# A hybrid encoder layer on one core: gate weight splits re-timed, one transfer chain moved to GpSimd's queue, a table load moved, and two token tiles of the closing norm done otherwise

## The chip, the cores and the metric

The kernel runs on one core of a Trainium2 chip. The core has five engines that run their own instruction lists in order and meet at semaphores: TensorE (PE in the profile; PEld is its weight loading), VectorE (DVE), ScalarE (ACT), GpSimd (POOL) and SyncE (SP), which here only issues transfers. Sixteen DMA engines move data between the chip's memory (DRAM) and the core's. The metric is the device time of one execution in microseconds (us); the time of a kernel is the median of its runs.

## The reference

One encoder layer on 1024 tokens of width 1024, all in float32:

```
u = x @ W_in                                  # rq rk rv rg | aq ak av
y_ret = silu(rg) * groupnorm(retention_fwd(rq,rk,rv) + retention_bwd(rq,rk,rv)) * gn_gain   # 8 heads of 64
y_att = windowed attention of aq on ak, av    # 8 query heads, 2 kv heads, +-128 tokens, ALiBi, a sink logit
h = LN1(alpha * x + [y_ret, y_att] @ W_out)
f = (silu(h @ W_gate) * (h @ W_up)) @ W_down + sigmoid(h @ W_pg) * (p @ W_pe)   # hidden width 2816
out = LN2(alpha * h + f)
```

Retention is done in chunks of 128 tokens with a running state of 64x64 for each head and direction; groupnorm takes mean and variance over the 64 numbers of a head. The two layer norms take mean and variance over a token's 1024 numbers, with eps 1e-5, a gain and a bias.

## The kernel before

**Arithmetic.** Float32 products are made from halves: `split` copies a number to its rounded `hi` on ACT (type fp32r) and subtracts to get `lo` on DVE (L71, L72). A product of two split operands is three matmuls, hi*hi, hi*lo and lo*hi (`mm3`, L77 to L79). Later stages use Strassen's seven products for a 2x2 block product, so their weights are needed as sums and differences of blocks, each split in turn.

**Order.** The first part (to about 342 us) is written as a list of steps for PE; TensorE's list follows it, and a scheduler lines up what the other engines get. It runs the input projection as a filler: every triple of projection matmuls is a *tick* (0.68 us of PE). `take(k)` (L283) issues k ticks and, at every tick, those steps whose due tick has come from two lists, `side` and `later`. So a table of ticks says where a side job's instructions fall among the others. A pair of retention heads and the attention heads beside it make a stage; the first retention pair takes 48 ticks (120.5 to 163.1 us), and the second pair, with the second attention pair beside it, the next 48 (163.1 to 221.9 us).

**The gate's splits.** The weight of the embedding gate (W_pg) is needed much later, as seven split block sums for each of four row blocks k. `presplit_gate` (L645) makes them ahead of time in these two stages: `load(k)` (L651, transfers at L653) brings two tiles `pre` of 512 KB; each of seven steps may first add blocks on DVE (L663), then `put` (L601) copies to one of two tiles `pro` on ACT (L602), subtracts on DVE (L603), and stores 512 KB from SP's queue into `pgd` (L604). A step can only begin once the tile `pro` of two steps ago has been stored. `load(2)` goes with the first step of k=1, and `load(3)` has a place of its own in the table `at`.

**Retention's norm.** For each pair i and half hh of the tokens, `norm` (L494) sums squares over heads on PE, and DVE makes a row `kv` of two heads (L500). The reciprocal root is then made in five steps with due ticks 3, 6, 9, 12 and 15 ahead (`LAGS`): `spread` (two transfers of 2 KB that lay the row over partitions, `sn`), `power` on GpSimd (L508), `store` (4 KB to `rnd` in DRAM, L511), `fetch` (two broadcasting transfers of 128 KB into `kv1` or `rb`, L515), and `scaled` on DVE, which multiplies the retention output `y` (L519). All transfers are issued by SP. `qq` and `pt` are key operands, scaled on DVE (L411) and used by PE (L428); the same tiles hold squares (L489, L490 evicts the output).

**Attention.** `scores` makes a block's scores and softmax (`sc`), `turn` transposes them on PE (L572), ACT evicts them to `ptr` (L574), and `values` multiplies with the values (L584).

**The out-projection** follows at about 342 us. Its left operands are sums of the `y` tiles (`H`, `h`, `h0a`, by `split` and by additions at L870 to L876), its weights come split from `wod` by SP (L814). ACT evicts the first products into `h0b` (L972). The retention gate (L722 to L724) closes `y` of the last pair there.

**The feed-forward part** from about 545 us is written in units (`gunits`), with `ahead_g` issuing the preparation of operands for coming units. `post` evicts products to `ev` tiles on ACT (L1424, L1426) or adds them on DVE (L1417), and `finish` applies silu on ACT (L1388) and multiplies on DVE (L1390). ACT holds the functions of one table at a time and has to load another to change (`ACT_TABLE_LOAD`). L1854 calls silu once on one number, which brings a load of its table there; the sigmoid of the embedding gate (L1097) comes after it.

**The tail.** The last products complete token tiles 0 to 3 one after the other (`tail`, L1683); tiles 4 to 7 are finished before, by `ln2_steps`. For tiles 0 to 3 the layer norm on tile `accd[t]` (128 tokens) goes: `addto` adds the last product; with `done` also sums the tile's half, on DVE within the same instruction (L1618) or, for a half that is subtracted into, on ACT (L1624); `var` makes the negative mean (L1630) and squares on ACT (L1635); `rstd` makes the reciprocal root by a power on GpSimd (L1652); `center` subtracts the mean and multiplies by the gain in one DVE instruction per half (L1657); `scale` multiplies by the reciprocal root and adds the bias, again one DVE instruction per half, and stores each half (256 KB) from SP's queue (L1662, L1663). Only tile 3 (`LAST`) takes its statistics by `bn_stats` and `bn_aggr` on DVE (L1622, L1641) instead. Tiles 4 to 7 are scaled on ACT (L1674), multiplied by the gain on DVE (L1677), and their bias is added by an accumulating transfer on GpSimd's queue (L1678).

Of the kernel before, what the change touches and what calls it, by code (L numbers as in the profile page):

```python
# [11 lines left out]
AF = mybir.ActivationFunctionType  # L12
# [10 lines left out]
NPAIR = 4  # L23
# [19 lines left out]
def layer(tc, xT, xn, w_first, w_mt, w_rv, w_out, w_pg, w_pe, pT, w_gu, w_dn,  # L43
# [349 lines left out]
    class Retention:  # L393
# [100 lines left out]
        def norm(self, hh):  # L494

            b = self.o.rearrange("p n c -> p (n c)")
            for k in range(2):
                pe.matmul(b, ones, self.sq[k], start=k == 0, stop=k == 1)
            row = bt([2, HF], "kv0")
            behind(dve.tensor_scalar(row, b[0:2], 1.0 / 64, EPS, ALU.mult, ALU.add))  # L500
            sm, r, home = bt([P, 2, 8], "sn", 1), bt([P, HF], ("kv1", "rb")[hh]), rnd[2 * self.i + hh]

            def spread():
                for h in range(2):
                    sp.dma_start(sm[64 * h:64 * h + 64, 0], row[h:h + 1].rearrange("o (q e) -> o q e", e=8))

            def power():
                behind(pool.tensor_tensor(sm[:, 1], sm[:, 0], cst[:, C_MH:C_MH + 1].to_broadcast([P, 8]), ALU.pow))  # L508

            def store():  # L510
                sp.dma_start(home, sm[:, 1])  # L511

            def fetch():
                for h in range(2):
                    sp.dma_start(r[64 * h:64 * h + 64], home[64 * h:64 * h + 64].rearrange("q e -> (q e)").partition_broadcast(64))  # L515

            def scaled():
                y = self.half(hh)
                behind(dve.scalar_tensor_tensor(y, y, gn[:, self.i:self.i + 1], r, ALU.mult, ALU.mult))  # L519

            later.extend((ticks[0] + at, f) for at, f in zip(LAGS, (spread, power, store, fetch, scaled)))
# [123 lines left out]
    def presplit_gate():  # L645

        first, other = ([a_tile([P, 2, HF], "pre", t) for _ in range(2)] for t in ("A1", "A0"))
        ops = [a_tile([P, 2, HF], "pro", "A1", F32R) for _ in range(2)]
        n = [0]

        def load(k):  # L651
            for j in range(2):
                sp.dma_start((other if k == 1 else first)[j], w_pg[j, k])  # L653

        def steps(k):
            raw = other if k == 1 else first

            (a11, a21), (a12, a22) = ([raw[j][:, i, :] for i in range(2)] for j in range(2))

            def s(p, x, *sums):  # L660
                def f():
                    for a in sums:
                        behind(dve.tensor_tensor(*a))  # L663
                    put(x, ops[n[0] % 2], pgd[p - 1, k])
                    n[0] += 1
                return f

            return [s(1, a11), s(4, a22), s(2, a12), s(5, a22, (a22, a21, a22, ALU.add)),
                    s(7, a21, (a21, a11, a21, ALU.subtract)), s(6, a11, (a11, a22, a11, ALU.subtract)),
                    s(3, a12, (a12, a12, a11, ALU.subtract))]  # L670

        load(0)
        load(1)
        k0, k1, k2, k3 = map(steps, range(4))
        k1[0] = pair_of(k1[0], lambda: load(2))
        k3[0:0] = [lambda: load(3), lambda: None]
        at = [2 + 3.4 * k for k in range(12)] + [55 + 2.5 * k for k in range(2)] + [65 + 1.9 * k for k in range(7)] + \
            [78.5 + 2 * k for k in range(9)]
        return [(ticks[0] + t, f) for t, f in zip(at, k0 + k1 + k2 + k3, strict=True)]

    def pair_of(f, g):
# [932 lines left out]
    def addto(t, h, b, op=ALU.add, done=False):  # L1614


        if done and t != LAST and op == ALU.add:
            dve.tensor_tensor_reduce(half(t, h), half(t, h), b, 1.0, 0.0, op, ALU.add, stts[t][:, h:h + 1])  # L1618
            return
        dve.tensor_tensor(half(t, h), half(t, h), b, op)  # L1620
        if done and t == LAST:
            dve.bn_stats(stts[t][:, 6 * h:6 * h + 6], half(t, h))  # L1622
        elif done:
            act.activation(ct([P, HF], "sg", 2), half(t, h), AF.Copy, accum_out=stts[t][:, h:h + 1])  # L1624

    LAST = 3

    def negmean(t):
        stt = stts[t]
# [7 lines left out]
    def var(t):  # L1637

        stt = stts[t]
        if t == LAST:  # L1640
            dve.bn_aggr(stt[:, 12:14], stt[:, 0:12])  # L1641
            dve.tensor_scalar(stt[:, 12:13], stt[:, 12:13], -1.0, None, ALU.mult)
        else:
            negmean(t)
            squares(t)

    def rstd(t):
        stt = stts[t]
        if t != LAST:
            dve.tensor_scalar(stt[:, 13:14], stt[:, 2:3], stt[:, 3:4], 1.0 / D, ALU.add, ALU.mult)  # L1650
        dve.tensor_scalar(stt[:, 14:15], stt[:, 13:14], EPS, None, ALU.add)
        pool.tensor_tensor(stt[:, 15:16], stt[:, 14:15], cst[:, C_MH:C_MH + 1], ALU.pow)  # L1652

    def center(t):
        for h in range(2):
            x = half(t, h)
            dve.scalar_tensor_tensor(x, x, stts[t][:, 12:13], ln2[0][:, hs[h]], ALU.add, ALU.mult)  # L1657

    def scale(t):
        for h in range(2):  # L1660
            x = half(t, h)
            dve.scalar_tensor_tensor(x, x, stts[t][:, 15:16], ln2[1][:, hs[h]], ALU.mult, ALU.add)  # L1662
            sp.dma_start(out[t][:, hs[h]], x)  # L1663
# [18 lines left out]
    def tail(products):  # L1682

        bs = dbank[len(SEG) - 1, GRP[4]]
        for t in range(4):
            products(t)
            if t:
                rstd(t - 1)
            addto(t, 0, bs[t], done=True)
            var(t)  # L1690
            if t < LAST:
                if t:
                    scale(t - 1)
                center(t)
        rstd(LAST)
        scale(LAST - 1)
        center(LAST)
        scale(LAST)

    GRP = {1: 0, 2: 0, 5: 1, 3: 1, 6: 2, 7: 2, 4: 2}  # L1700

# [137 lines left out]
    with tc.manual_schedule(engines={ET.PE, ET.DVE, ET.Activation, ET.Pool, ET.SP}):  # L1839
        for _ in range(4):  # L1840
            oslots.append(wp.tile([P, 2, HF], F32R, tag="w", bufs=4, name=nm("w")))
            oslots.append(ct([P, 2, HF], "u", 4, F32R))
        sums2.extend(a_tile([P, 2, HF], "sums") for _ in range(2))
        fa = big16((P, 4, 2, 2, Q))
        halves4 = [(fa[:, k, 0], fa[:, k, 1]) for k in range(4)]
        halves4.append(tuple(ct([P, 2, Q], "sg", 2, F32R) for _ in range(2)))
        fsum.extend([cst[:, 0:Q], cst[:, Q:2 * Q], *(ct([P, Q], "fs", 2) for _ in range(2))])
        fwide = ct([P, 2, Q], "p", 2)
        fine, more = fine_right(2, halves4[:3]), fine_right(4, halves4[3:])
        fine += more  # L1850
        homes.update((name, a_tile([P, 2, HF], "ev")) for name in ("spare", "s1", "u2", "c11", "u3", "c22"))
        FINE4 = len(plan(0)) + len(plan(1)) - 2
        FINES = (2, 4, 7, 9, 20, 23, 26, FINE4)
        act.activation(fsum[3][:, 0:1], fsum[0][:, 0:1], AF.Silu)  # L1854
        ahead_g(-1, 4)
        for k in range(NG):
            gunits[k][1]()
            gunits[k][2]()
            if k in FINES:
                at = max([-1] + [i for i, x in enumerate(items) if x.right]) + 1  # L1860
                for x in fine.pop(0):
                    at += 1
                    x.unit, x.right = items[at].unit, True
                    items.insert(at, x)
                    at += 1
            ahead_g(k, k + 1 + min(9, 4 + k))
            while stores and stores[0][0] <= k:
                stores.pop(0)[1]()
            j = k + 1 - NG
            if j == -6:  # L1870
                while items:
                    items.pop(0).issue()
                release()
                arenas_a()
                op_arena(ct([P, 4, 2, HF], "h0a", dt=F32R))
                arena("chain", ct([P, 8, HF], "h0b"), 8)
            if j == -4:
                for _ in range(3):
                    op_arena(big16((P, 4, 2, HF)))
            if j >= -6:  # L1880
                ahead(0, j + 7)
            if j >= -4:
                ahead(1, j + 5)
        arena("b", big.tile([P, 8, HF], F32, tag="H", bufs=4, name=nm("H")), 8)
        arena("chain", ct([P, 8, HF], "h2"), 8)
        op_arena(ct([P, 4, 2, HF], "h3", dt=F32R), 4)
        rings["op"] += [ct([P, 2, HF], "u", 4, F32R) for _ in range(2)]
        for k in range(ND):
            d_step(k)
# [83 lines left out]
```

## Time and profile before

| | us |
|---|---|
| runs | 1169.49, 1171.92, 1171.9 |
| median | 1171.9 |
| profiled execution, its own time | 1172.7 |
| its span | 1170.6 |
| granted TensorE clock, mean | 0.998 |

The profile is of one execution. An engine's busy time says little here: PE is nearly always busy, and what is left are the places where it waits, the start, and the end of the span where PE has finished. A timeline row gives start, length, engine, line, operation, output<-inputs, shapes and how many rows it joins, and in brackets the idle time ahead of it with what ended it. `pgd`, `wod`, `rnd`, `ped` are places in DRAM; `w<-wod` is a transfer from there.

### The profile page before, as it was taken

Reading aid. Unit: us, or ns where it says so; the run is one execution under the profiler, and the core shown is the slowest. Engines: PE = TensorE matmul, PEld = TensorE weight load, DVE = VectorE, ACT = ScalarE, POOL = GpSimd, SP = SyncE. Lnnn points to the kernel's source line nnn. Section 1 sums busy time; section 2 is a strip of 40 time slices with the busy share of each in tenths; the row PEclk is TensorE's granted clock in tenths of the full one; section 3 lists DMA queues with packets and bytes.
Section 4 is the critical chain, followed back from the end, with each engine's and each line's share of the span. In section 5 each row is a group of like instructions: output and inputs, shape, how many; then the busy total and the mean of one; then the engine's idle time right before and its main releaser. Section 6 shows DMA issues by size and latency. Waiting matters only on the chain.

```text
span 1170.6 us, 17933 instructions
## 1 busy us (share of the span) xinstructions
PE 1156.5 (99%) x6330; PEld 971.5 (83%) x6330; DVE 900.4 (77%) x1746; ACT 580.1 (50%) x1181; POOL 121.0 (10%) x181
## 2 busy tenths in 40 slices
PE   9999999999999999999999999999999999999996
PEld 7888888788887888888888888888888888888885
DVE  4666688777869688947998988888888976773677
ACT  5566348686756256214445434443344445552463
POOL 2001021202010021000000000000000020133232
PEclk9999999999999999999999999999999999999999
DMA  6345665746356955665322222232223289999977
GB/s 252 100 153 207 246 207 193 244 159 223 127 190 230 365 172 196 261 195 201 117 90 105 112 105 100 102 135 101 99 72 136 89 249 349 350 225 203 261 173 216
DMA packets 84378, 213.86 MB, mean 183 GB/s; under 512 B 12225, under 2 KB 17473, under 8 KB 84289
## 3 DMA queue, kind: packets, MB, share of 16 engines
q1 hardware_dynamic: 75648, 195.94, 47.6%
q0 software_dynamic: 8640, 16.78, 8.2%
q8 instruction: 50, 0.82, 0.3%
q14 instruction: 40, 0.32, 0.1%
HBM read 141.32 MB, written 62.16 MB: 174 GB/s over the span
## 4 chain that ended last, share of the span: by engine, by line
PE 86%; DVE 6%; DMA 4%; ACT 2%; issue 1%; POOL 0%; SPq 0%; DVEq 0%; ACTq 0%; POOLq 0%
PE bmm L803 8%; PE bmm L804 8%; PE bmm L805 7%; PE bt L803 6%; PE bt L804 6%; PE bt L805 6%; PE bmm L77 4%; PE bs L803 4%; PE bs L805 4%; PE bs L804 4%; PE bmm L79 4%; PE bmm L78 4%; PE bo L805 3%; PE bo L803 3%; PE bo L804 3%
## 5 line engine op out<-in xcount | busy, mean ns | idle before, releaser
L77 PE MATMUL bmm<-H,w 128*128 128x512 f32 x240 | 97.3, 405 | 0.0
L78 PE MATMUL bmm<-H,w 128*128 128x512 f32 x240 | 93.9, 391 | 0.0
L79 PE MATMUL bmm<-H,w 128*128 128x512 f32 x240 | 93.9, 391 | 0.0
L1388 ACT ACTIVATE ev<-ev 128x512 f32<-128x512 f32 x42 | 26.5, 630 | 104.3 <-DVE ev L1417 92.8
L1562 POOL DMA_DIRECT2D h0b<-in_w_dn x24 | 21.6, 899 | 540.7 <-DVE ev L1368 504.9
L77 PEld LDWEIGHTS bmm<-H,w 128*128 128x128 f32 x240 | 45.1, 188 | 11.1 <-issue 1.4
L79 PEld LDWEIGHTS bmm<-H,w 128*128 128x128 f32 x240 | 45.1, 188 | 10.3
L78 PEld LDWEIGHTS bmm<-H,w 128*128 128x128 f32 x240 | 45.2, 188 | 7.9
L554 ACT ACTIVATE sc<-sc,st 128x385 f32<-128x385 f32 (+1 forms) x64 | 37.2, 585 | 15.6 <-DVE st L552 15.3
L550 DVE CUSTOM_DVE_ANT_0 sc<-cst,bs,skb 128x384 f32<-128x384 f32 (+1 forms) x64 | 35.0, 575 | 8.3 <-PE bs L549 7.8
L1417 DVE TENSOR_TENSOR ev<-ev,bt 128x512 f32<-128x512 f32 x44 | 30.1, 683 | 12.5 <-PE bt L805 12.5
L1368 DVE TENSOR_TENSOR ev<-ev,bs 128x256 f32<-128x256 f32 x63 | 25.6, 418 | 15.5 <-PE bs L805 14.7
L1390 DVE TENSOR_TENSOR ev<-ev 128x512 f32<-128x512 f32 x42 | 29.0, 691 | 10.5 <-ACT ev L1388 9.0
L803 PE MATMUL bmm<-H,u 128*128 128x512 f32 x92 | 36.2, 393 | 0.2 <-ACT ev L1426 0.2
L804 PE MATMUL bmm<-H,u 128*128 128x512 f32 x92 | 36.0, 392 | 0.0
L805 PE MATMUL bmm<-H,u 128*128 128x512 f32 x92 | 35.8, 389 | 0.0
L72 DVE TENSOR_TENSOR w<-raw,w 128x512 fp32r<-128x512 f32 x34 | 23.1, 688 | 16.2 <-ACT w L71 16.1
L545 POOL COPY sc<-skb 128x1 f32<-128x1 f32 x64 | 15.6, 253 | 188.9 <-PE bt L572 144.5
L560 ACT ACTIVATE sc<-sc,st 128x384 f32<-128x384 f32 (+1 forms) x64 | 34.2, 580 | 1.2 <-DVE st L558 0.9
L71 ACT ACTIVATE H<-ln 128x512 fp32r<-128x512 f32 (+1 forms) x34 | 22.7, 675 | 21.2 <-DVE ln L1052 7.2
L803 PE MATMUL bmm<-H,w 128*128 128x512 f32 x84 | 32.9, 392 | 0.0
L804 PE MATMUL bmm<-H,w 128*128 128x512 f32 x84 | 32.9, 392 | 0.0
(802 smaller groups left out, 3898.4 us busy)
## 6 DMA issues: line engine op xcount, KB each, us to landing
ad<-ev SPq DMA_DIRECT2D x33, 512.0 KB, 2.6
pgd<-pro SPq DMA_DIRECT2D x28, 512.0 KB, 3.0
raw<-in_w_gu SPq DMA_DIRECT2D x22, 512.0 KB, 3.6
ln<-in_w_gu SPq DMA_DIRECT2D x22, 512.0 KB, 3.9
raw<-ad SPq DMA_DIRECT2D x40, 256.0 KB, 5.6
ln<-ad SPq DMA_DIRECT2D x37, 256.0 KB, 6.0
H<-in_w_dn SPq DMA_DIRECT2D x33, 256.0 KB, 7.4
wod<-aq SPq DMA_DIRECT2D x15, 512.0 KB, 2.8
```

The costliest lines, as they stand in the source:

```text
L77: pe.matmul(o, lh, rh, start=start, stop=False)
L78: pe.matmul(o, lh, rl, start=False, stop=False)
L79: recent[0] = pe.matmul(o, ll, rh, start=False, stop=stop).ins.name
L550: dve.tensor_tensor_reduce(sc[g][:, :nk], cst[:, tc0:tc0 + nk], b[:, :nk], slope(i, g), skb[:, 2 * i + g:2 * i + g + 1], ALU.add, ALU.max, ...
L554: act.activation(sc[g][:, :nk + 1], sc[g][:, :nk + 1], AF.Exp, bias=st_[:, 1, j, g:g + 1], accum_out=st_[:, 2, j, g:g + 1])
L560: behind(act.activation(sc[g][:, :nk], sc[g][:, :nk], AF.Copy, scale=st_[:, 3, j, g:g + 1]))
L803: pe.matmul(o, lh, rh, start=start, stop=False, skip_group_check=True)
L804: pe.matmul(o, lh, rl, start=False, stop=False, skip_group_check=True)
L805: pe.matmul(o, ll, rh, start=False, stop=stop, skip_group_check=True)
L1388: act.activation(c[:, 0, :], c[:, 0, :], AF.Silu)
L1390: dve.tensor_tensor(c[:, 1, :], c[:, 0, :], c[:, 1, :], ALU.mult)
L1417: dve.tensor_tensor(get(name), ev[left][:, m, :], right, ALU.add)
```

## The change

The edits lie in four parts of the kernel. None touches what PE does.

```diff
+            q = pool if hh and self.i == NPAIR - 1 else sp
...
             def store():
-                sp.dma_start(home, sm[:, 1])
+                q.dma_start(home, sm[:, 1])
 
             def fetch():
                 for h in range(2):
-                    sp.dma_start(r[64 * h:64 * h + 64], home[64 * h:64 * h + 64].rearrange("q e -> (q e)").partition_broadcast(64))
+                    q.dma_start(r[64 * h:64 * h + 64], home[64 * h:64 * h + 64].rearrange("q e -> (q e)").partition_broadcast(64))
...
         k3[0:0] = [lambda: load(3), lambda: None]
-        at = [2 + 3.4 * k for k in range(12)] + [55 + 2.5 * k for k in range(2)] + [65 + 1.9 * k for k in range(7)] + \
-            [78.5 + 2 * k for k in range(9)]
+        at = [2 + 2.8 * k for k in range(14)] + [60 + 1.9 * k for k in range(7)] + [73 + 1.9 * k for k in range(9)]
...
-        if done and t != LAST and op == ALU.add:
+        if done and t not in BN and op == ALU.add:
...
-        if done and t == LAST:
+        if done and t in BN:
             dve.bn_stats(stts[t][:, 6 * h:6 * h + 6], half(t, h))
...
-    LAST = 3
+    LAST, BN = 3, (2, 3)
...
         for t in range(4):
             products(t)
-            if t:
+            if t in (1, 2):
                 rstd(t - 1)
             addto(t, 0, bs[t], done=True)
             var(t)
-            if t < LAST:
-                if t:
-                    scale(t - 1)
-                center(t)
-        rstd(LAST)
-        scale(LAST - 1)
-        center(LAST)
-        scale(LAST)
+            if t in BN:
+                rstd(t)
+            if t == 1:
+                scale(0)
+            elif t == 2:
+                act.activation(accd[1], accd[1], AF.Copy, scale=stts[1][:, 15:16])
+                pool.dma_start(accd[1], ln2[1], accum_op=ALU.add)
+            center(t)
+            if t in BN:
+                scale(t)
+            if t == 2:
+                sp.dma_start(out[1], accd[1])
...
-        act.activation(fsum[3][:, 0:1], fsum[0][:, 0:1], AF.Silu)
         ahead_g(-1, 4)
         for k in range(NG):
...
             ahead_g(k, k + 1 + min(9, 4 + k))
+            if k == 0:
+                act.activation(fsum[3][:, 0:1], fsum[0][:, 0:1], AF.Silu)
```

Line numbers in the rows of after are those of the changed file, one to five higher. `var` and `rstd` ask for `t in BN` where they asked for `t == LAST`.

**Gate's splits.** The table has 30 places, counted in ticks from 120.5 us on. Before: 12 from tick 2 to 39.4, two at 55 and 57.5, seven from 65 to 76.4, nine (the first two of them `load(3)` and an empty place) from 78.5 to 94.5. After: 14 from 2 to 38.4, seven from 60 to 71.4, nine from 73 to 88.2. So two of the splits move from the second stage into the first, and the last ends six ticks earlier.

DVE where the second stage hands over to the third, up to the key operand `pt` of the third, before:

```order
L603 TENSOR_TENSOR pro_1168<-pre_1163,pro_1168 128x512
L663 TENSOR_TENSOR pre_1164<-pre_1164,pre_1163 128x512
L519 SCALAR_TENSOR_TENSOR y_1596<-y_1596,gn,kv_2110 128x512
L251 SCALAR_TENSOR_TENSOR aq_2236<-bmm_2242,aq_2236 64x512
L411 TENSOR_TENSOR qq_2330<-bt_2325,kd 128x512
L603 TENSOR_TENSOR pro_1167<-pre_1163,pro_1167 128x512
L251 SCALAR_TENSOR_TENSOR aq_2237<-bmm_2242,aq_2237 64x512
L411 TENSOR_TENSOR qq_2330<-bt_2325,kd 128x512
L603 TENSOR_TENSOR pro_1168<-pre_1164,pro_1168 128x512
L72 TENSOR_TENSOR w_2335<-raw_2333,w_2335 128x512
L72 TENSOR_TENSOR w_2338<-raw_2333,w_2338 128x512
L411 TENSOR_TENSOR pt_2360<-bt_2355,kd 128x512 x2
```

And after:

```order
L665 TENSOR_TENSOR pre_1164<-pre_1164,pre_1163 128x512
L251 SCALAR_TENSOR_TENSOR aq_2249<-bmm_2125,aq_2249 64x512
L605 TENSOR_TENSOR pro_1168<-pre_1164,pro_1168 128x512
L500 TENSOR_SCALAR kv_2288<-bo_2201 2x512
L72 TENSOR_TENSOR w_2335<-raw_2333,w_2335 128x512
L521 SCALAR_TENSOR_TENSOR y_1604<-y_1604,gn,kv_2116 128x512
L411 TENSOR_TENSOR qq_2330<-bt_2325,kd 128x512
L251 SCALAR_TENSOR_TENSOR aq_2248<-bmm_2254,aq_2248 64x512
L411 TENSOR_TENSOR qq_2330<-bt_2325,kd 128x512
L72 TENSOR_TENSOR w_2338<-raw_2333,w_2338 128x512
L251 SCALAR_TENSOR_TENSOR aq_2249<-bmm_2254,aq_2249 64x512
L411 TENSOR_TENSOR pt_2360<-bt_2355,kd 128x512 x2
```

The rows of `pro` and `pre` have moved ahead. From the eviction `y` (L490), which stands further up in both, to `pt` there are 20 rows before and 14 after.

ACT where the second attention block of the second stage has its two transposes evicted (`ptr`, 128x384), before:

```order
L235 ACTIVATE rk_1726<-bmm_1728 128x512
L574 ACTIVATE ptr_1828<-bt_1824 128x384
L560 ACTIVATE sc_1776<-sc_1776,st_1635 128x384
L560 ACTIVATE sc_1777<-sc_1777,st_1635 128x384
L574 ACTIVATE ptr_1834<-bt_1830 128x384
L554 ACTIVATE sc_1836,st_1635<-sc_1836,st_1635 128x385
```

And after:

```order
L235 ACTIVATE rk_1730<-bmm_1732 128x512
L562 ACTIVATE sc_1779<-sc_1779,st_1643 128x384
L562 ACTIVATE sc_1780<-sc_1780,st_1643 128x384
L576 ACTIVATE ptr_1837<-bt_1833 128x384
L604 ACTIVATE pro_1167<-pre_1164 128x512
L576 ACTIVATE ptr_1843<-bt_1839 128x384
L556 ACTIVATE sc_1845,st_1643<-sc_1845,st_1643 128x385
```

Both scalings `sc` and a split (`pro`) now stand ahead of the second eviction, the scalings ahead of the first too.

**The last factor.** Only for the last pair's second half, `store` and `fetch` are issued by GpSimd. SP's list there, before:

```order
L505 DMA sn_3719<-kv_3717 64x1x8 x2
L511 DMA rnd<-sn_3719 128x8
L604 DMA ped<-aq_3046 128x1024
L515 DMA rb_3720<-rnd 64x512 x2
L814 DMA u_3835<-wod 128x1024
L814 DMA w_3837<-wod 128x1024
```

And after:

```order
L507 DMA sn_3719<-kv_3717 64x1x8 x2
L606 DMA ped<-aq_3046 128x1024
L815 DMA u_3835<-wod 128x1024
L815 DMA w_3837<-wod 128x1024
L815 DMA u_3839<-wod 128x1024
```

The weights `wod` follow directly on `ped`; the three transfers of the factor stand on GpSimd's list behind its power. On DVE one of the splits `H<-y,H` now stands ahead of the `y` that takes the factor (L519), and the second of the additions L876 is the 26th row behind `y` where it was the 28th.

**Silu's table.** The one-number silu goes from ahead of all units to behind the first. Before, ACT loads silu's table at L1854, the sigmoid's at L1097 and silu's again at L1388; after, the sigmoid's and then silu's once, between two evictions at L1425.

**The closing norm.** Tile 2 takes its statistics like tile 3, and goes through `center` and `scale` ahead of tile 3. Tile 1 is no longer scaled on DVE: ACT scales it (128x1024), GpSimd's queue adds the bias by an accumulating transfer, and SP stores it whole (512 KB), behind tile 2's stores and ahead of tile 3's. DVE's last rows before:

```order
L1662 SCALAR_TENSOR_TENSOR acc_8948<-acc_8948,stt_3931,u_9976 128x512 x2
L1657 SCALAR_TENSOR_TENSOR acc_8976<-acc_8976,stt_3932,u_9974 128x512 x2
L1650 TENSOR_SCALAR stt_3932<-stt_3932 128x1
L1651 TENSOR_SCALAR stt_3932<-stt_3932 128x1
L1620 TENSOR_TENSOR acc_9000<-acc_9000,bs_9954 128x512
L1622 BN_STATS stt_3933<-acc_9000 128x6
L1641 BN_AGGR stt_3933<-stt_3933 128x2
L1642 TENSOR_SCALAR stt_3933<-stt_3933 128x1
L1651 TENSOR_SCALAR stt_3933<-stt_3933 128x1
L1662 SCALAR_TENSOR_TENSOR acc_8976<-acc_8976,stt_3932,u_9976 128x512 x2
L1657 SCALAR_TENSOR_TENSOR acc_9000<-acc_9000,stt_3933,u_9974 128x512 x2
L1662 SCALAR_TENSOR_TENSOR acc_9000<-acc_9000,stt_3933,u_9976 128x512 x2
```

And after:

```order
L1642 BN_AGGR stt_3932<-stt_3932 128x2
L1643 TENSOR_SCALAR stt_3932<-stt_3932 128x1
L1652 TENSOR_SCALAR stt_3932<-stt_3932 128x1
L1658 SCALAR_TENSOR_TENSOR acc_8976<-acc_8976,stt_3932,u_9974 128x512 x2
L1663 SCALAR_TENSOR_TENSOR acc_8976<-acc_8976,stt_3932,u_9976 128x512 x2
L1621 TENSOR_TENSOR acc_9000<-acc_9000,bs_9954 128x512
L1623 BN_STATS stt_3933<-acc_9000 128x6
L1642 BN_AGGR stt_3933<-stt_3933 128x2
L1643 TENSOR_SCALAR stt_3933<-stt_3933 128x1
L1652 TENSOR_SCALAR stt_3933<-stt_3933 128x1
L1658 SCALAR_TENSOR_TENSOR acc_9000<-acc_9000,stt_3933,u_9974 128x512 x2
L1663 SCALAR_TENSOR_TENSOR acc_9000<-acc_9000,stt_3933,u_9976 128x512 x2
```

Tiles 1, 2 and 3 are `acc_8948`, `acc_8976` and `acc_9000`. The scaling of tile 2 (L1662) has moved from between tile 3's statistics and its centring to ahead of tile 3's addition, and tile 1's is gone.

More of the change, by code (lines that the diff above doesn't have):

```diff
@@ L1639, in var @@
         stt = stts[t]
-        if t == LAST:
+        if t in BN:
             dve.bn_aggr(stt[:, 12:14], stt[:, 0:12])
@@ L1648, in rstd @@
         stt = stts[t]
-        if t != LAST:
+        if t not in BN:
             dve.tensor_scalar(stt[:, 13:14], stt[:, 2:3], stt[:, 3:4], 1.0 / D, ALU.add, ALU.mult)
@@ L1690, in tail @@
             var(t)
-            if t < LAST:
-                if t:
-                    scale(t - 1)
-                center(t)
-        rstd(LAST)
-        scale(LAST - 1)
-        center(LAST)
-        scale(LAST)
+            if t in BN:
[6 more added lines that the diff above has]
+            center(t)
+            if t in BN:
+                scale(t)
+            if t == 2:
+                sp.dma_start(out[1], accd[1])
     GRP = {1: 0, 2: 0, 5: 1, 3: 1, 6: 2, 7: 2, 4: 2}
```

## The prediction

> **What bounds the kernel.** I read the head of the page first, then the PE waits, then the stretches. In the stretches the columns are length, PE, PE loads, DVE, ACT, POOL, clock, DMA share, GB/s.
>
> ```profile
> span 1170.6 us, 17933 instructions
> PE 1156.5 (99%) x6330; PEld 971.5 (83%) x6330; DVE 900.4 (77%) x1746; ACT 580.1 (50%) x1181; POOL 121.0 (10%) x181
> ...
> PE bt L428 <- DVE pt L411: 2.0, 1, 2.0
> ...
> PE bs L803 <- ACT h0b L972: 0.6, 1, 0.6
> PE bt L803 <- DMA u<-wod: 0.4, 1, 0.4
> ...
> PE bt L572 <- ACT ptr L574: 0.3, 1, 0.3
> PE bmm L803 <- ACT ev L1426: 0.2, 1, 0.2
> ...
> 342.00:376.00 34.00, 32.90 (x155) 25.66 (x155) 26.39 (x43) 19.76 (x35) 1.64 (x1) 1.00 0.59 210
> ...
> 1150.00:1170.60 20.60, 11.76 (x52) 9.39 (x51) 15.65 (x36) 4.57 (x12) 3.05 (x5) 0.90 0.69 219
> ```
>
> TensorE is busy 99% of the span, and the change leaves its instructions and their order alone. So only two things can move the time: the waits of PE, five of which (2.0, 0.6, 0.4, 0.3, 0.2: 3.5 us) lie where the change works, and the tail of some 9 us in the last stretch in which PE has nothing left. The most to be had is those 3.5 us and a piece of the tail.
>
> **The gate's splits.** The 2.0 us wait stands where retention's second pair hands over to the third.
>
> ```profile
> 213.19 0.63 ACT L602 ACTIVATE pro<-pre 128x512 fp32r<-128x512 f32 x1 [0.98 <-DMA pre<-in_w_pg]
> 222.92 0.63 ACT L602 ACTIVATE pro<-pre 128x512 fp32r<-128x512 f32 x1 [1.18 <-DMA pgd<-pro]
> ...
> 216.19 0.69 DVE L490 COPY y<-bo 128x512 f32<-128x512 f32 x1 [1.65 <-ACT pt L489]
> ...
> 230.73 1.28 DVE L411 TENSOR_TENSOR pt<-bt,kd 128x512 f32<-128x512 f32 x2
> ...
> 232.16 1.04 PE L428 MATMUL bt<-rv,pt 128*64 128x64 f32 x28 [1.97 <-DVE pt L411]
> ```
>
> PE waits for `pt`, and DVE is late with it because it works through a queue: ACT sat twice behind the last weight tile's load and store (0.98 and 1.18), and between `y` at 216.19 and `pt` at 230.73 DVE has 20 instructions, of which 9 are the splits' own (`pro`, `pre`). In the new order it has 14, with 3 of these. Six less at the 0.6 us by which such rows follow one another (two take 1.28, one 0.69) let `pt` begin at 227.1 and end at 228.4; PE, which came 1.97 before 232.16, comes for it at 230.2, so 1.8 are to spare. The last load is issued 5.5 ticks earlier, 6.7 us at the 58.8 us that this stage takes for 48 ticks, so its landing is no longer in the way. I take the whole wait, -2.0; the ends are -2.0 and -0.5 (if only a quarter of those rows' time is really ahead of `pt`).
>
> What that work meets further up:
>
> ```profile
> 168.62 1.29 DVE L411 TENSOR_TENSOR pt<-bt,kd 128x512 f32<-128x512 f32 x2
> 170.19 0.99 PE L428 MATMUL bt<-rv,pt 128*64 128x64 f32 x28
> ...
> 181.84 0.88 PE L572 MATMUL bt<-cst,sc 128*128 128x128 f32 x6 [0.28 <-ACT ptr L574]
> ...
> 185.01 0.49 ACT L574 ACTIVATE ptr<-bt 128x384 f32<-128x384 f32 x1
> ...
> 185.42 1.31 PE L584 MATMUL bo<-ptr,av 128*64 128x128 f32 x20
> ```
>
> Two more splits fall in the first pair's stage. At its end `pt` is ready at 169.91, 0.28 before PE takes it at 170.19; there DVE has 13 rows ahead of it instead of 12, though it begins earlier: +0.1 (0 to +0.5). At 181.84 PE's 0.28 goes, since the splits leave that stretch. But a split (0.63 of ACT) now stands between the two evictions of one attention block, and the two 128x384 scalings ahead of both: the second `ptr`, done at 185.50 now, is done at about 186.1, and PE is there 0.3 earlier. I take a new wait of 0.8, net +0.5 (-0.3 to +0.9). The 28 stores and 4 pairs of loads stay; on SP's queue two of the stores now stand ahead of the first norm's round trip, whose last step is 1 us later with nothing close behind: 0. Together -1.4.
>
> **The last factor on GpSimd's queue.**
>
> ```profile
> 347.05 0.33 SPq L511 DMA_DIRECT2D rnd<-sn  x1
> ...
> 348.49 1.11 SPq L515 DMA_DIRECT2D rb<-rnd  x2
> 349.65 0.58 SPq L814 DMA_DIRECT2D u<-wod  x1
> ...
> 353.06 0.75 DVE L519 SCALAR_TENSOR_TENSOR y<-y,gn,rb 128x512 f32<-128x512 f32 x1 [1.62 <-DMA rb<-rnd]
> 353.73 3.69 DVE L72 TENSOR_TENSOR H<-y,H 128x512 fp32r<-128x512 f32 x6
> ...
> 373.07 0.50 PE L803 MATMUL bs<-w,H 128*128 128x512 f32 x1 [0.55 <-ACT h0b L972]
> ```
>
> SP issues `u<-wod` at 349.65 only because the factor's two steps stand ahead; without them it goes out behind `ped` about 3 us earlier and PE's 0.4 for it is gone. That alone buys nothing: PE waits again at 373.07, for ACT's eviction behind a split (`h0a`) that takes what DVE made, and DVE's timeline names no idle time from `y` at 353.06 to there. So the term is how much earlier DVE gets through `y`. The addition (L876) that this split of ACT takes is the 28th row behind `y` now and the 26th in the new order, and rows are 0.6 apart (six take 3.69); so `y` may start as late as 353.06 + 1.2 = 354.26 without loss. The factor's store and the two fetches now cost POOL three issues of 0.90 (below) instead of SP's 0.33 and 0.55 each. If a GpSimd transfer lands as SP's do, `rb` is there at 353; if each of the two steps takes 1.5 us longer, at 356. I take 353.9, nearer to the first, since the transfers are small and POOL has nothing else: -0.4. Ends: -0.9 (both waits; the stretch from 342 has 1.10 without PE in all) and +1.7.
>
> **Silu's table.** A load leaves ACT at 362.84, where ACT was waiting for DVE anyway (0), and another moves from 549.79 to some 4 us earlier.
>
> ```profile
> 549.79 1.28 ACT L1388 ACT_TABLE_LOAD   x1 [2.41 <-DVE ev L1417]
> ...
> 558.09 0.50 PE L803 MATMUL bmm<-H,u 128*128 128x512 f32 x1 [0.20 <-ACT ev L1426]
> ```
>
> The 2.41 ahead of the load is idle, so 1.28 + 0.2 of work fit in; behind it ACT and DVE hand to each other until `ev` at 558.09, now 1.28 earlier: -0.2. Were the cover gone, it would be 0.
>
> **The tail.** The first landing row is that of the accumulating transfers, the second that of the last eight stores.
>
> ```profile
> L1678 POOL DMA_DIRECT2D acc<-u  x4: 859/894/913, 1140.8 to 1149.6; - x4
> ...
> DMA to landing us min/median/max: 4.5/4.9/8.5
> ...
> DMA to landing us min/median/max: 2.0/2.4/3.0
> ...
> 1140.80:1145.30 4.50, 4.50 (x22) 3.72 (x21) 3.47 (x8) 3.61 (x6) 3.96 (x5) 1.00 0.60 118
> 1144.10:1148.60 4.50, 4.50 (x21) 3.72 (x21) 4.38 (x7) 3.57 (x7) 1.85 (x4) 1.00 0.87 197
> 1148.40:1153.80 5.40, 5.40 (x25) 4.46 (x25) 3.56 (x9) 2.10 (x6) 2.17 (x3) 1.00 1.03 288
> 1149.60:1158.10 8.50, 8.50 (x39) 7.06 (x38) 6.82 (x17) 3.05 (x8) 1.86 (x3) 1.00 0.93 240
> ...
> 1157.72 0.69 DVE L1618 CUSTOM_DVE_ANT_0 acc<-acc,bs 128x512 f32<-128x512 f32 x1 [0.18 <-PE bs L805]
> ...
> 1163.79 0.98 POOL L1652 TENSOR_TENSOR stt<-stt,cst 128x1 f32<-128x1 f32 x1 [1.55 <-DVE stt L1651]
> ...
> 1161.80 0.69 DVE L1620 TENSOR_TENSOR acc<-acc,bs 128x512 f32<-128x512 f32 x1 [0.18 <-PE bs L805]
> ...
> 1163.62 1.40 DVE L1662 SCALAR_TENSOR_TENSOR acc<-acc,stt,u 128x512 f32<-128x512 f32 x2
> 1164.94 1.41 DVE L1657 SCALAR_TENSOR_TENSOR acc<-acc,stt,u 128x512 f32<-128x512 f32 x2
> 1166.27 1.41 DVE L1662 SCALAR_TENSOR_TENSOR acc<-acc,stt,u 128x512 f32<-128x512 f32 x2
> ```
>
> From the last addition to a tile's first big pass is 1.82 us (1161.80 to 1163.62), and a pass of two takes 1.32. Before, the last tile goes through that and three passes, one of them the third tile's scaling, and begins its own at 1166.27. In the new order the third tile does all of its own first: 1157.72 + 1.82 + 2 x 1.32 = 1162.2, 0.4 later than 1161.80; the last then needs 1.82 + 1.32, so its scaling begins at 1165.3, 0.9 earlier. But the second tile's scaling is now an ACT pass, an accumulating transfer on GpSimd, and one store on SP's queue ahead of the last tile's two. GpSimd reaches that transfer behind the third tile's power (from 1159.6, 0.98 long) at about 1160.7; at 4.5 it lands at T = 1165.2. Until T the last stores can't go, and they are ready at 1166.1 and 1166.7. I take 4.5 since two rows have it and the DMA share in their stretches (0.60, 0.87) is the nearer to this one, from which the second tile's old stores leave; 5.4 and 8.5 came at 1.03 and 0.93. With the store of 512 KB just ahead of them they lose part of their 0.9: -0.5. Ends: -0.9, and at 8.5 (T = 1169.2) about +3.
>
> By the rows, with T = 1165.2, the tail gives the -0.5 above. The Trainium skill speaks against both moves to GpSimd ("SBUF — State Buffer", "SBUF: two separate sides"): descriptors of GpSimd's DMAs are written by its cores, which are kept off a port pair shared with VectorE during some VectorE instructions; it advises SP's or ACT's queue. By that rule alone the transfer would wait for the passes' end and the sum would be that of the first rival below. Here landing took 4.5 both with DVE busy 3.47 of 4.50 us and with 4.38, so the rows go with the DMA share instead; but the power at 1163.79, beside the passes, took 0.98.
>
> **Sum.** -1.4 - 0.4 - 0.2 - 0.5 = -2.5 us. The profiled execution took 1172.7 for its span of 1170.6, 0.8 over the median of the runs, and would go to 1170.2; the median 1171.9 goes to 1169.4. A measurement of this kernel tells 0.2%, 2.3 us, from no change, so the forecast lies just past that bound.
>
> **Rivals.**
> - Slower: the accumulating transfer comes late and blocks SP's queue, because its descriptors wait until DVE's passes end at 1166.7. With 4.5 less the issue of 0.9 still to come, T = 1170.3, and the stores behind it land some 3.9 us after T (2.6 for the first, between the median and the slowest, and 0.65 for each of the two behind it, the spacing of the passes), at 1174.2; now the last leaves at 1167.7 and lands 2.0 later, at 1169.7. That is 4.5 more. With -2.0 of the rest: +2.5, 1174.4. It costs from T = 1165.8 on and eats the whole gain at T = 1168. For it: 8.5 is in the rows, and the 0.98. Against it: the 4.5 beside 4.38 of DVE.
> - The splits' own waits: in denser order they make PE wait at `pt` near 170 and at `ptr` near 186 for 0.5 and 0.9, and `pt` at 230 is still 0.8 late. Then they bring -0.1: 1170.7.
> - `rb` lands at 356: DVE stands at `y`, the wait at 373 grows, +1.7 instead of -0.4: 1171.5.
> - Everything at its good end: -2.3 - 0.9 - 0.2 - 0.9 = -4.3, 1167.6. For it: the new `ptr` wait is the least certain term.
>
> **How the numbers follow.** Forecast 0.50, with an own range of 1168.3 to 1170.5 of which six tenths lie past the bound; good ends 0.20; splits' waits 0.10; late factor 0.07; blocked stores 0.13. Faster 0.30 + 0.20 + a little of the others' spread = 0.53; slower 0.13 + 0.02; same 0.32. The range goes from 1166.6, past the good end, to 1173.2, which leaves out the blocked stores and little else.
>
> **What would show it.** PE's waits: no `bt <- pt` of 2.0, at most 1 us at `ptr` near 185, none for `u<-wod`, none for `ev` near 558. `y` starts before 354.3 (less what was gained earlier). The accumulating transfer lands within 5 us and the last store leaves by 1167. A wait for `pt` that stays, `y` after 355, or a landing over 8 us would make it wrong.

## The result, and the profile after

The changed kernel takes 1176.95 us in the median (1175.70 to 1178.61, 4 runs) against 1170.7 of the kernel before in the same comparison: a ratio of 1.0056, with a 95% interval from 1.0034 to 1.0078. It is 0.56% slower; the forecast was 1169.4 with an upper end of 1173.2. PE's waits in the profiled execution after (its span 1176.7, its own time 1178.61; each line gives the us in total, how many waits, and the longest):

```profile
PE bt L806 <- DVE H L72: 6.6, 1, 6.6
...
PE bt L804 <- ACT h0b L973: 1.2, 1, 1.2
PE bs L550 <- DVE pt L461: 0.8, 1, 0.8
PE bt L574 <- ACT ptr L576: 0.4, 1, 0.4
```

The waits of 2.0 (`pt`, L411), 0.4 (`u<-wod`) and 0.2 (`ev`) are gone, and one of 6.6 has come. Where, and what DVE was doing (timeline of after, DVE and PE):

```profile
351.28 0.69 DVE L72 TENSOR_TENSOR H<-y,H 128x512 fp32r<-128x512 f32 x1
...
360.96 0.75 DVE L521 SCALAR_TENSOR_TENSOR y<-y,gn,rb 128x512 f32<-128x512 f32 x1 [8.99 <-DMA rb<-rnd]
361.63 3.10 DVE L72 TENSOR_TENSOR H<-y,H 128x512 fp32r<-128x512 f32 x5
...
362.37 0.79 PE L806 MATMUL bt<-u,H 128*128 128x512 f32 x1 [6.58 <-DVE H L72]
362.96 0.63 PE L804 MATMUL bt<-w,H 128*128 128x512 f32 x1
...
364.67 0.63 PE L805 MATMUL bt<-u,H 128*128 128x512 f32 x1
```

DVE stands 9 us at the `y` that takes the last factor, and the splits PE needs are behind it in DVE's order. The transfers of that stretch (issued from 338 to 354.5; size and median us from issue to landing), before and then after:

```profile
u<-wod SPq DMA_DIRECT2D x3, 512.0 KB, 6.7
...
rb<-rnd SPq DMA_DIRECT2D x2, 128.0 KB, 3.7
...
rnd<-sn SPq DMA_DIRECT2D x1, 4.0 KB, 1.4
```

```profile
u<-wod SPq DMA_DIRECT2D x3, 512.0 KB, 6.5
...
rb<-rnd POOLq DMA_DIRECT2D x2, 128.0 KB, 6.3
...
rnd<-sn POOLq DMA_DIRECT2D x1, 4.0 KB, 6.0
```

The store took 6.0 instead of 1.4 and the fetches 6.3 instead of 3.7, which is 7.2 of the 7.9 us by which `y` starts later. To say where the rest of the time went, the start of each TensorE matmul is compared with that of the same matmul before, with the offset at 120 us taken off (the starts differ by up to 0.9 from one execution to the next). In us, minus is earlier; each column is one execution:

| at (us of before) | after | e1 no factor | e2 factor alone | e7 gate alone | e9 tie on before | e8 tie, no factor |
|---|---|---|---|---|---|---|
| 222 | +0.3 | -0.6 | -0.5 | +0.5 | -0.7 | -0.9 |
| 240 | -0.9 | -1.8 | -0.5 | -0.4 | -1.5 | -3.4 |
| 340 | -0.6 | -1.1 | -0.2 | 0.0 | -1.9 | -3.8 |
| 380 | +6.9 | -1.8 | +6.5 | +0.5 | -3.4 | -5.5 |
| 540 | +6.3 | -2.4 | +6.0 | +0.2 | -3.0 | -4.8 |
| 570 | +5.8 | -2.8 | +5.9 | +0.1 | -3.2 | -5.3 |
| 1160 | +5.6 | -3.0 | +6.0 | +0.1 | -3.1 | -5.5 |

### The profile page after: what moved, and what is told of

Read it like the earlier page. It is cut to its first block, busy times and chain, and to the rows that moved or that the text cites. A ratio compares the mean times of both kernels' runs of the same rounds, so it can differ in the third digit from the quotient of the medians.

```text
span 1176.7 us, 17921 instructions
## 1 busy us (share of the span) xinstructions
PE 1157.6 (98%) x6330; PEld 973.4 (83%) x6330; DVE 902.4 (77%) x1745; ACT 577.1 (49%) x1175; POOL 123.3 (10%) x185
## 4 chain that ended last, share of the span: by engine, by line
PE 89%; DVE 5%; DMA 3%; ACT 2%; issue 1%; SPq 0%; POOL 0%; DVEq 0%; ACTq 0%; POOLq 0%
PE bmm L804 8%; PE bmm L805 8%; PE bmm L806 8%; PE bt L804 6%; PE bt L805 6%; PE bt L806 6%; PE bmm L77 5%; PE bmm L78 4%; PE bmm L79 4%; PE bs L806 4%; PE bs L805 4%; PE bs L804 4%; PE bo L806 4%; PE bo L805 4%; PE bo L804 4%; PE bo L586 1%
## 5 line engine op out<-in xcount | busy, mean ns | idle before, releaser
L77 PE MATMUL bmm<-H,w 128*128 128x512 f32 x240 | 97.3, 405 | 0.0
L78 PE MATMUL bmm<-H,w 128*128 128x512 f32 x240 | 94.1, 392 | 0.0
L79 PE MATMUL bmm<-H,w 128*128 128x512 f32 x240 | 93.9, 391 | 0.0
L576 ACT ACTIVATE ptr<-bt 128x384 f32<-128x384 f32 (+1 forms) x64 | 26.5, 457 | 13.5 <-PE bt L574 13.4
L804 PE MATMUL bmm<-H,w 128*128 128x512 f32 x84 | 32.9, 392 | 0.0
```

What stands on the lines that cost most here:

```text
L77: pe.matmul(o, lh, rh, start=start, stop=False)
L78: pe.matmul(o, lh, rl, start=False, stop=False)
L79: recent[0] = pe.matmul(o, ll, rh, start=False, stop=stop).ins.name
L576: act.activation(p_[:, :hi - lo, :], tb[:, :hi - lo, :], AF.Copy)
L804: pe.matmul(o, lh, rh, start=start, stop=False, skip_group_check=True)
```

## The experiments

Two theories on the last factor. **G**: a transfer on GpSimd's queue needs over 4 us by itself. **W**: taking the factor's two steps off SP's queue lets the out-projection's weights, 512 KB each, go ahead; before, they stood behind the fetch and could not start until the store had landed, so the store had the DMA engines nearly to itself (busy 0.16 of its flight) and the fetches were ahead of the weights. Under W the queue that issues the factor doesn't matter.

**e1: the factor back on SP's queue.**

```diff
-            q = pool if hh and self.i == NPAIR - 1 else sp
+            q = sp
```

> The changed kernel with the last factor's store and fetch back on SP's queue; gate's splits, silu's table and the closing norm stay changed. Theory F (the factor is the whole loss): PE's wait of 6.6 us near 355 is gone, what is left there is the 0.4 and 0.6 of before; the time is that of before less 0.6 (splits) less 0.4 (silu) less 0.6 (tail), a ratio of 0.9986, between 0.9975 and 1.000. Rival (the splits or the tail lose too): 1.001 or more.

1170.87 us against 1171.53, ratio 0.9992 (0.9983 to 1.0001). Its PE waits:

```profile
PE bt L804 <- ACT h0b L973: 1.2, 1, 1.2
PE bs L550 <- DVE pt L461: 0.8, 1, 0.8
PE bt L574 <- ACT sc L562: 0.2, 1, 0.2
```

The whole loss is the factor's; the other three parts together bring some 0.9 us, and by the interval it could be nothing. The wait of 1.2 at `h0b`, where 0.6 was expected, is here without the move as well.

**e2: the factor alone on the kernel before.** The same lines as in the change, nothing else.

> The kernel before with only the last factor's store and fetch on GpSimd's queue. Theory F: y L519/L521 starts about 361, PE waits some 6.6 us near 355, and the time is 7.5 us over before, a ratio of 1.0064 (1.005 to 1.008). Rival (it needs the other parts, the earlier splits for instance): less than 1.003.

1178.87 us, ratio 1.0062 (1.0045 to 1.0079). The fetches land in 6.2 us, `y` starts at 359.80, PE waits 5.9. It needs none of the other parts.

**e3: the weights held until the store has landed.**

```diff
             def fetch():
+                if q is pool:
+                    sp.dma_start(sm[:, 0], home)
```

> The changed kernel with one more transfer of 4 KB on SP's queue, which reads the stored factor back into a tile that is not used any more: SP's weights for the out-projection then wait until the store has landed, as they did before the change. Theory G (a transfer on GpSimd's queue needs over 4 us by itself): the store still lands 4.2 to 4.5 us after its issue, the fetch 4.5 to 6 after its own, and y starts at 357 to 358. Theory W (the small transfers are late because 2 MB of weights now fly beside them): the store lands in 1.4 to 2 us and y starts near 354.

```profile
rb<-rnd POOLq DMA_DIRECT2D x2, 128.0 KB, 5.8
...
rnd<-sn POOLq DMA_DIRECT2D x1, 4.0 KB, 2.5
```

One run, 1175.71 us. On the same queue the store now lands in 2.5 us instead of 6.0, which G can't give, though W had said at most 2. The fetches, with the weights released ahead of them, still take 5.8, and `y` starts at 357.11, which is within G's range and 3 us behind W's: only half of the chain was freed, and this run alone doesn't decide.

**e4: the factor on ACT's queue, weights as in the changed kernel.**

```diff
-            q = pool if hh and self.i == NPAIR - 1 else sp
+            q = act if hh and self.i == NPAIR - 1 else sp
```

> The changed kernel with the last factor's store and fetch on ACT's queue instead of GpSimd's; the weights go ahead on SP's as in the changed kernel. Theory G: the store lands 1.4 to 2.5 us after issue, the fetch 3.5 to 5, y starts at about 353.5, and the time is that of e1 or up to 0.5 us less. Theory W: the weights beside them delay them as on GpSimd's queue: 5 to 6 us each, y near 360, ratio about 1.005.

1176.89 us, ratio 1.0041 (1.0025 to 1.0058).

```profile
rb<-rnd ACTq DMA_DIRECT2D x2, 128.0 KB, 7.3
...
rnd<-sn ACTq DMA_DIRECT2D x1, 4.0 KB, 4.9
```

And while the store flies, in the stretches:

```profile
347.30:352.20 4.90, 4.90 (x24) 4.04 (x23) 0.00 (x0) 0.00 (x0) 0.00 (x0) 1.00 0.98 307
```

The DMA engines are busy 0.98 of that time (second number from the right), as they are in after while its store flies. `y` starts at 361.12. The slowness doesn't belong to GpSimd.

**e5: the weights held until the fetches have landed too.** Behind the fetch on GpSimd's queue, SP reads eight columns of each half of `rb` back, so its weights wait for it:

```diff
                     q.dma_start(r[64 * h:64 * h + 64], home[64 * h:64 * h + 64].rearrange("q e -> (q e)").partition_broadcast(64))
+                if q is pool:
+                    for h in range(2):
+                        sp.dma_start(sm[64 * h:64 * h + 64, 0], r[64 * h:64 * h + 64, 0:8])
```

> The changed kernel with two small transfers on SP's queue that read the fetched factor back into a tile not used any more: SP's weights for the out-projection now wait until the whole factor has landed. By theory W (the weights beside them make the factor's transfers late; GpSimd's queue itself costs about 1.1 us for each step): the store lands about 2.5 us after issue, the fetches 3 to 4.5, y starts at 353 to 354, near the 353.1 of before, and PE now waits 2 to 4 us for the weights instead. By theory G the fetches need 4.2 or more with nothing beside them and y starts at 355 or later.

```profile
rb<-rnd POOLq DMA_DIRECT2D x2, 128.0 KB, 3.0
...
rnd<-sn POOLq DMA_DIRECT2D x1, 4.0 KB, 2.5
```

The stretches in which the store and the fetches fly, and the largest PE wait:

```profile
345.20:347.70 2.50, 2.50 (x13) 2.07 (x12) 0.00 (x0) 0.60 (x1) 0.76 (x1) 1.00 0.45 177
348.20:351.80 3.60, 3.60 (x17) 2.98 (x17) 1.58 (x3) 3.34 (x7) 1.06 (x2) 1.00 0.24 73
```

```profile
PE bt L807 <- DMA u<-wod: 4.1, 1, 4.1
```

One run, 1174.04 us. With the DMA engines at 0.45 and 0.24, GpSimd's fetches land in 3.0, sooner than SP's 3.7 before; `y` starts at 351.84, over 1 us before W's range. PE now waits 4.1 for the weights that were held. W stands, G falls.

What is left of the store's delay, 2.5 against the 1.4 of before, doesn't belong to GpSimd either. In e3 and e5 a `ped` of 512 KB is issued 1 us ahead of the store, where before it went out 0.4 behind it. In e8 and e9 below `ped` goes out 0.65 ahead of a store on SP's queue, and SP's store takes as long (e8, then e9):

```profile
rnd<-sn SPq DMA_DIRECT2D x1, 4.0 KB, 2.6
```

```profile
rnd<-sn SPq DMA_DIRECT2D x1, 4.0 KB, 2.3
```

What counts is what was issued ahead, more than how busy the DMA engines are: in e1 they are busy 0.98 of the time while SP's fetches fly (346.81 to 351.10), with the weights behind, and the fetches take 4.3.

**e6: only the fetches on GpSimd's queue.** `store` uses `sp`, `fetch` uses `q`.

> The changed kernel with the store back on SP's queue and only the two fetches on GpSimd's. Three weights go out behind the store while it is under way, as in the changed kernel. Theory W: the store lands in under 2 us, the fetches, issued near 348, share the DMA engines with 1.5 MB and land 5 to 7 us later; y at 353.5 to 355 and PE waits 0.5 to 2 us. If only GpSimd's own 1.1 us counts: fetches in 4.5, y at 352.5, no more waiting than with both on SP.

One run, 1174.67 us: the store on SP lands in 1.4, the fetches in 7.2 beside three weights (DMA share 0.99), `y` at 356.19, PE waits 3.5. The landings agree with W's to 0.2; `y` is 1.2 us later and the wait 1.5 longer than its ranges allow. The chain in one view (us to landing as above; "held" means that SP's weights stand behind the factor):

| | store | fetches | `y` starts | longest PE wait there |
|---|---|---|---|---|
| before: SP, held | 1.4 | 3.7 | 353.06 | 0.6 |
| after: GpSimd, weights beside | 6.0 | 6.3 | 360.96 | 6.6 |
| e4: ACT, weights beside | 4.9 | 7.3 | 361.12 | 7.1 |
| e6: SP then GpSimd, weights beside the fetches | 1.4 | 7.2 | 356.19 | 3.5 |
| e3: GpSimd, held for the store | 2.5 | 5.8 | 357.11 | 3.6 |
| e5: GpSimd, held for both | 2.5 | 3.0 | 351.84 | 4.1, for the weights |

**e7: the gate's table alone on the kernel before.**

> The kernel before with the new table of the gate's splits alone. Theory: PE's wait of 2.0 us near 230 goes, waits of 0.5 near 207 and of 0.8 to 1.0 near 236 come; from 120 us to 340 us the program gains 0.5 to 0.7 us against before, and nothing changes behind it. Rival (the waits at 207 and 236 belong to the other parts): it gains 2 us or more.

```profile
PE bs L548 <- DVE pt L461: 1.1, 1, 1.1
PE bt L572 <- ACT ptr L574: 0.8, 1, 0.8
```

One run. The wait of 2.0 is gone and these two have come; at 340 us nothing is gained, where 0.5 to 0.7 was expected. The second is near 207, the first near 236. In after, around the first (DVE and PE; `kv` here are the state updates of retention's scan):

```profile
228.29 1.29 DVE L411 TENSOR_TENSOR pt<-bt,kd 128x512 f32<-128x512 f32 x2
...
230.45 0.99 PE L428 MATMUL bt<-rv,pt 128*64 128x64 f32 x28
...
234.07 0.28 DVE L441 SCALAR_TENSOR_TENSOR kv<-kv,cd 128x64 f32<-128x64 f32 x1
...
234.85 1.28 DVE L461 TENSOR_TENSOR pt<-bs,dt 128x512 f32<-128x512 f32 x2
...
235.60 0.45 PE L550 MATMUL bs<-k,aq 128*128 128x384 f32 x1 [0.80 <-DVE pt L461]
```

`pt` for the keys is ready at 229.6, 0.9 before PE takes it. But four state updates (234.07 to 234.85, 0.8 us; one of them in the order before) now run ahead of the score products that free PE's bank.

**e8: the state updates tied behind TensorE's projection in the order**, on e1's kernel. In `scan`:

```diff
-                dve.scalar_tensor_tensor(U[0][:, n, :], U[0][:, n - 1, :], cd[:, i:i + 1], U[0][:, n, :],
-                                         ALU.mult, ALU.add)
+                behind(dve.scalar_tensor_tensor(U[0][:, n, :], U[0][:, n - 1, :], cd[:, i:i + 1], U[0][:, n, :],
+                                         ALU.mult, ALU.add))
```

and the same for `U[1]`.

> The changed kernel with the factor on SP's queue, and the state updates of retention's scan tied behind TensorE's projection in the order: on DVE four of them no longer stand ahead of the two score products pt near 234 us. Theory S (those four rows of 0.2 us make PE's new wait of 0.8): the wait near 234 is gone, 0.7 to 0.9 us gained over the same kernel without it, a ratio to before of 0.9985 (0.997 to 1.000). Rival: the later states make PE wait at retention's output instead, and nothing is gained.

1166.43 us (1165.75 to 1166.94), ratio 0.9955 (0.9941 to 0.9969): faster than both kernels, and by more than expected. Its score products and the matmul behind them:

```profile
230.63 1.28 DVE L461 TENSOR_TENSOR pt<-bs,dt 128x512 f32<-128x512 f32 x2
...
232.51 0.33 PE L550 MATMUL bs<-k,aq 128*128 128x384 f32 x1
```

The wait near 236 is gone, so that the wait at 230 is won whole: 2.5 us from 222 to 240 in the table, where e1 won 1.2. The rest was not taken apart; what the trace shows is that the last factor's store is issued at 340.94 instead of e1's 345.37, and that `y` waits for nothing.

**e9: the same tie on the kernel before.**

> The kernel before with nothing changed but the tie of the scan's state updates. If the gain of e8 over e1 is the tie's alone and adds to what is there: splits, silu and tail still cost their 1 to 2 us here, the wait of 2.0 near 230 stays, and the ratio to before is 0.997 to 0.9985, slower than e8. If the changed parts bring nothing once the tie is there: as fast as e8, 0.9955.

1169.51 us, ratio 0.9977 (0.9968 to 0.9986). PE's wait near 230 stays, at 1.5. So splits, silu and tail bring 0.22% together once the tie is there: 2.6 us (0.6 to 4.5, from the intervals of e8 and e9) where the forecast had 2.1 for them, and where without the tie they bring 0.08%.

**e10: the tie on the changed kernel, factor on GpSimd's queue.**

> The changed kernel, factor on GpSimd's queue as it was changed, with the tie of the scan's state updates. The last factor is ready some 4 us earlier than in the changed kernel, but so are the weights that go past it on SP's queue. Theory W: store and fetch again fly beside 1.5 to 2 MB of weights and take 5 to 7 us each, y starts at 351 to 354 instead of 347.7, and the time is 3 to 6 us over that of e8, ratio to before 0.998 to 1.001. If the early start is enough to hide them: within 1 us of e8.

1174.57 us, ratio 1.0021 (1.0013 to 1.0030).

```profile
rb<-rnd POOLq DMA_DIRECT2D x2, 128.0 KB, 5.3
...
rnd<-sn POOLq DMA_DIRECT2D x1, 4.0 KB, 6.2
```

Though the store is issued at 342.08, the weights go 0.6 us ahead of it; `y` starts at 355.54, 1.5 us later than expected, and PE waits 5.1. Against e8 the move costs 0.0066, 7.7 us, where 3 to 6 was expected: the same as in e2 within the intervals. An earlier start doesn't hide it.

## Why the prediction was wrong

**The last factor: forecast -0.4, measured +7.5** (340 to 380 us in the column of after). The step that failed: "If a GpSimd transfer lands as SP's do, `rb` is there at 353; if each of the two steps takes 1.5 us longer, at 356." Both ends took the transfers' duration as a property of the queue. It goes with what flies ahead of them and beside them, and that was changed by the move itself: the prediction saw that `u<-wod` "goes out behind `ped` about 3 us earlier", asked whether that gains anything, and charged nothing for it. Three weights of 512 KB are 1.5 MB; the store and the fetches are 4 and 256 KB. With these and a `ped` ahead of them the two steps took 4.6 and 2.6 us longer, in place of the 1.5 each of the bad end. The rows for it stood in the prediction's own tail part, where landings of 4.5 went with a DMA share of 0.60 and 0.87, and 5.4 and 8.5 with 1.03 and 0.93.

The way from a late `y` to PE was another than the prediction's, too. The prediction's went over the addition L876 and ACT's eviction to the wait at 373, and so let `y` start as late as 354.26. (The addition is the 30th row behind `y` in the trace and the 28th in the new order, not the 28th and 26th; the difference of two is right.) What stopped PE lay nearer: from 355.79 it waited for a split `H` that is the first row behind `y` in DVE's order. Before, PE came by this place without a wait (the second row):

```profile
355.54 0.39 PE L804 MATMUL bt<-u,H 128*128 128x512 f32 x1
355.77 0.39 PE L805 MATMUL bt<-u,H 128*128 128x512 f32 x1
```

On this way `y` could start until 354.38 in after (360.96 less the wait of 6.58); that 354.26 lies so near is luck. The wait alone puts PE some 6.7 behind. A lower clock after it (below) and the wait of 1.2 at `h0b` add to this, and the waits of 0.4 and 0.6 of before are no longer paid, which makes 7.5. So the rival "`rb` lands at 356" had DVE standing at `y` right, but at a quarter of the cost, with a chance of 0.07, and with neither the reason nor the wait that was measured.

The Trainium skill says it under "DMA: Bandwidth & Descriptors", "Issuing engines are not separate DMA queues": transfers of all issuing engines run on the same 16 DMA engines and interleave. e4 agrees: ACT's store of 4 KB took 4.9 us beside the weights. The rule I weighed instead, of the port shared with VectorE, is not what acted: DVE was idle from 345.9 to 349.9, when GpSimd issued the store (346.92), and for the 8.99 us ahead of `y`, when it issued the fetches (353.44).

**The gate's splits: forecast -1.4, measured about -0.6** (after -0.6, e1 -1.1, e7 0.0, in executions that scatter by half a us). The 2.0 went as said, with `pt` beginning at 228.29 where 227.1 was forecast. The new wait at 186 did not come. Two others did, of up to 0.8 near 207 and 0.5 to 1.1 near 236, because the prediction did not ask what is late next once PE no longer stands 2 us at 230 while DVE catches up. In e8, which ties all of the scan's state updates and not only the four, the second is gone.

**Silu's table: forecast -0.2, measured -0.3 to -0.4** (540 to 570 is -0.4 to -0.5 in after, e1 and e8, and -0.1 to -0.2 in e2, e7 and e9, which lack it). The mechanism held; that it is a little more than the wait was not taken apart.

**The tail: forecast -0.5, measured -0.5 to -0.6 to the last landing, and -0.3 in the span.** In after, the accumulating transfer by its line, and then DVE's last addition and scaling in the timeline:

```profile
L1698 POOL DMA_DIRECT2D acc<-u x1: 885/885/885, 1166.8 to 1166.8; - x1
...
DMA to landing us min/median/max: 4.5/4.5/4.5
```

```profile
1168.35 0.68 DVE L1621 TENSOR_TENSOR acc<-acc,bs 128x512 f32<-128x512 f32 x1
...
1171.56 1.41 DVE L1663 SCALAR_TENSOR_TENSOR acc<-acc,stt,u 128x512 f32<-128x512 f32 x2
```

The accumulating transfer lands 4.5 us after issue, as taken, at 1171.3, just ahead of the last scaling's first half. The last scaling begins 4.1 us after PE's last matmul (1167.46) instead of 4.9 (1161.37), and the last store lands 7.8 after it instead of 8.3; 7.7 to 7.8 in the eight kernels with the new tail, 8.3 in the four without. The closing steps behind it take 1.0 to 1.45 us in the eight and 0.9 to 1.1 in the four, so that in the mean only 0.3 of this reaches the span; whether the new tail lengthens them is not shown. The blocked stores did not come.

The sum without the factor was -2.1; e1 measures -0.9 with an interval from -2.0 to +0.1.

## What to carry to other kernels

A transfer that waits at the head of a queue also holds back everything behind it; before moving it to another queue, list what is then released, how many bytes that is, and which small latency-bound transfers they will meet on the DMA engines. A transfer's time is to be taken from rows with the like issued ahead of it and beside it; a like queue does not do, and a like DMA share alone does not either (0.98 with fetches of 4.3 in e1, 0.99 with 7.2 in e6). And when a wait is removed, look for what was catching up during it: here most of the 2 us came back further on, until the scan's small state updates were put behind.

## What was not expected of the hardware

After its long wait, PE ran slow: matmuls that start 0.23 us apart before it start 0.43 apart behind it, six of them in after (362.37 to 365.10), 12 in e2, 14 in e5 (357.3 to 363.0), which costs 1.4 to 2.9 us more. The granted clock shows it:

```profile
342.00:376.00 34.00, 26.23 (x123) 20.79 (x122) 19.16 (x31) 14.55 (x27) 3.48 (x4) 0.90 0.55 179
355.79:358.42 2.63, 0.00 (x1) 0.00 (x0) 0.00 (x0) 1.15 (x3) 0.00 (x0) 1.00 0.76 231
358.42:365.25 6.83, 2.88 (x7) 2.30 (x8) 4.29 (x8) 0.00 (x0) 0.00 (x0) 0.50 0.50 167
```

The clock (third number from the right) is 0.90 over the stretch of after and 1.00 before. PE stopped at 355.79; 2.63 us later the clock was halved, and it stayed so for 6.83 us, though PE worked again from 362.37. In e3, where PE stood from 354.93 to 358.52:

```profile
354.93:359.72 4.79, 1.20 (x5) 1.03 (x6) 2.61 (x5) 1.14 (x3) 0.00 (x0) 1.00 1.02 362
359.72:363.13 3.41, 3.41 (x9) 2.65 (x9) 3.41 (x6) 0.00 (x0) 0.00 (x0) 0.50 0.69 281
```

There the half clock came 1.2 us after PE had gone on, and lasted 3.41 us. The wait of 2.0 at 230 in the kernel before was followed by no such stretch; the shortest wait that was is e6's of 3.5. So a wait of a few us can cost more than its length. The Trainium skill ("TensorE: Matmul & The Clock Gate", "Part 1: The HAM clock gate") has the clock halved after about 3.4 us without work until the array has been busy again as long. The lengths here agree with one and two such times, 3.41 in e3 and 6.83 in after, e2, e4, e5, e6 and e10. The start does not agree with a count from PE's stop, which it follows by 2.2 us in e6, 2.6 in after and 4.8 in e3. So the length of a wait alone does not settle its price, and where the limit lies between 2.0 and 3.5 us is not shown.
